# A chunked recurrence: double levels taken apart into single ones that read q in place

## The chip, the cores and the metric

The kernel runs on one core of a Trainium2 chip. A core has five engines with their own instruction streams: PE (TensorE) multiplies matrices, with the loads of its stationary operand shown apart as PEld; DVE (VectorE), ACT (ScalarE) and POOL (GpSimd) work on vectors; SP (SyncE) issues transfers. The metric is the device time of one execution in microseconds (us).

## The reference

The network is one layer of a hybrid block over 2048 positions of width 1024: a normalisation, an input projection to 4608 columns, two branches (a pooling mixer and a gated recurrence), sigmoid gates, an output projection, a convolutional feed-forward part, and a last normalisation. All is fp32. The change touches only the recurrence, with 4 heads of 128 channels. Per head, with the state S (128 x 128):

```
f_t = lb + (1 - lb) * sigmoid(zf_t);   k_t = 1 - f_t;   q_t = silu(zq_t)
S_t = diag(f_t) S_{t-1} + k_t v_t^T
o_t = S_t^T q_t
```

Within a chunk of positions the same is an attention with a decay, summed over the channel c, for s <= t:

```
att[t, s] = sum_c q[t, c] * k[s, c] * f[s+1, c] * ... * f[t, c]
o = att @ v + (q * decay) @ S_of_the_chunk's_start
```

## The kernel before, in words

The 2048 positions are handled as two passes of 1024, and each pass as two blocks of 512 positions (`TB`). In a pass `proj_io` projects the values and the output gate, `mixer` does the other projections (14 units of 7 products, each 4 x 3 matmuls of 128 x 128 x 512, so 1176 matmuls), then the branch projections `pa` and `pb`, then the output rows (`wo`), and `ffn` follows. A weight is split in two fp32r parts, `ops` (L209 on ACT, L210 on DVE), ahead of its use.

The recurrence is `hgrn_task`, one generator for each block and head: 4 blocks x 4 heads = 16 tasks, of which up to three (`N_RUN`) run at once in each pass. Nothing there is a loop of its own. The projections count their matmuls, and at every sixth (`MM_PER_TICK`) a tick lets each task whose `yield n` has run out issue its next step. So a task's instructions lie among those of the projections on every engine. The final order is drawn by the tile framework's scheduler from the order of issue and a timing model. Each engine takes its instructions in order.

In a task the tiles are 128 channels by 512 positions, in four chunks of 128 (`NT`). `d` holds the decays f, `ks` holds k, `q` holds q, and `att` collects the attention of each chunk. The attention is built by levels. At level hh (1, 2, 4, ... 64) a chunk falls into pairs of neighbouring runs of hh positions; a product of `ks` (stationary, 128 columns) with the second runs' q (moving, 64 columns) gives all entries between the runs, a masked copy (`copy_predicated` on DVE, the mask as bytes) takes over the wanted ones into `att`, and then q of the second runs, k of the first runs and the decay of the run are multiplied forward, so that the next level has runs of twice the length. Level 64 needs no mask: its product has 64 stationary columns and ACT copies it (L925).

Before the change levels 0 and 1 (hh = 1, 2) work on copies of q: tiles `q1` and `q2` hold 64 columns for the level's pairs of runs and 64 for the diagonal of the even or the odd positions, side by side, and one product of 128 columns (L915) gives both. Levels 2 and 3, and levels 4 and 5, are done together by `two_levels`: for two chunks at a time, a tile `qm` of 3 x 64 columns gets the near runs (ACT, L867), the half-run copy (POOL, L868) and the multiplied far runs (DVE, L869 and L872), one product of 192 columns per chunk (L876) gives all, three masked copies take it over (L883, L886), and q, k and d go forward by two levels at once (L880, L892 to L898). Level 6 stands alone (L923). L933, L935 and L937 carry q, k and d forward by a single level. Between steps a task yields 3, 4, 4, then 1 + 1 + 5 for each double level, and 4 ticks: 29 up to its last product.

After that a task transposes k (`pk`), updates the state chunk by chunk (`pv`, `ss`), forms the output (`po`), normalises, transposes and spills it (`oh`, L987). The second block's task of a head waits for the first block's state. `pb` reads the spilled outputs. The masks are made by `setup_task` once, in the first pass, on POOL (L576 to L580) and DVE, while `proj_io` runs.

Of the kernel before, what the change touches and what calls it, by code (L numbers as in the profile page):

```python
# [78 lines left out]
def tile_trunk(  # L79
# [482 lines left out]
    def setup_task():  # L562
# [8 lines left out]
        keys = [(h, h, 0, h) for h in (1, 2, 4, 16)]  # L571
        keys += [(8 * h + t, 2 * h, t * h, h) for h in (4, 16) for t in range(2)]
        for key, x, off, w in keys:
            nb = 64 // x
            mf = slot(f"mf{key}", 64)
            pool.memset(mf, 1.0)  # L576
            v = mf.rearrange("p (b h) -> p b h", h=x)
            pool.affine_select(out=v, in_=v, pattern=[[-2 * x, nb], [0, x]],
                               compare_op=ALU.is_ge, fill=0.0, base=-off, channel_multiplier=1)
            pool.affine_select(out=v, in_=v, pattern=[[2 * x, nb], [0, x]],  # L580
                               compare_op=ALU.is_ge, fill=0.0, base=off + w - 1,
                               channel_multiplier=-1)
# [4 lines left out]
        for t in range(2):  # L587
            mf = slot(f"mfd{t}", 64)
            pool.memset(mf, 0.0)
            pool.affine_select(out=mf, in_=mf, compare_op=ALU.not_equal, fill=1.0, base=-t,  # L590
                               pattern=[[-2, 64]], channel_multiplier=1)
            m8 = const.tile([P, 64], U8, tag=f"md{t}", name=f"md{t}")
            yield 2
            dve.tensor_copy(m8, mf)
            masks[-1 - t] = m8.unsqueeze(1)
# [227 lines left out]
    def hgrn_task(b, h, d, q, vd, zd, od):  # L823
        def head_of(src, key):
# [13 lines left out]
        ae, ao = (att.rearrange("p (c b t) -> p c b t", c=NT, t=2)[:, :, :, t] for t in range(2))  # L838
# [4 lines left out]
        dve.tensor_tensor(q1[:, :, 0], qo, do, ALU.mult)  # L843
# [3 lines left out]
        def mask(key, n):  # L847
            m = masks[key]
            return m.unsqueeze(1).to_broadcast([P, n, m.shape[1], m.shape[2]])

        def two_levels(hh):
            nb = P // (4 * hh)
            d5 = d.rearrange("p (c b t h) -> p c b t h", c=NT, t=4, h=hh)
            q5 = q.rearrange("p (c b t h) -> p c b t h", c=NT, t=4, h=hh)
            qv = q.rearrange("p (c b t h) -> p c b t h", c=NT, t=2, h=hh)
            av = att.rearrange("p (c b t h) -> p c b t h", c=NT, t=2, h=hh)
            av2 = att.rearrange("p (c b t h) -> p c b t h", c=NT, t=2, h=2 * hh)
            q2 = q.rearrange("p (c b t h) -> p c b t h", c=NT, t=2, h=2 * hh)
            for i in range(0, NT, 2):
                cc = slice(i, i + 2)  # L860
                mv = (slot(f"qm{b}_{h}_{hh}_{i}")[:, :384]
                      .rearrange("p (c s x) -> p c s x", c=2, s=3))
                near = mv[:, :, 0].rearrange("p c (b h) -> p c b h", h=hh)
                half = mv[:, :, 1].rearrange("p c (b t h) -> p c b t h", t=2, h=hh)
                far = [mv[:, :, 1 + t].rearrange("p c (b h) -> p c b h", h=2 * hh)
                       for t in range(2)]
                act.copy(near, qv[:, cc, :, 1, :])  # L867
                pool.tensor_copy(half[:, :, :, 0, :], q5[:, cc, :, 2, :])  # L868
                dve.tensor_tensor(half[:, :, :, 1, :], q5[:, cc, :, 3, :],  # L869
                                  d5[:, cc, :, 2, 0:1].to_broadcast([P, 2, nb, hh]), ALU.mult)  # L870
                full = [P, 2, nb, 2 * hh]
                dve.tensor_tensor(far[1], far[0], d5[:, cc, :, 1, 0:1].to_broadcast(full),  # L872
                                  ALU.mult)
                pa_ = bank(f"pl{b}_{h}_{hh}_{i}", 384)
                for c in range(2):
                    pe.matmul(pa_[:, c * 192 : c * 192 + 192],  # L876
                              ks[:, (i + c) * P : (i + c + 1) * P],
                              mv[:, c].rearrange("p s x -> p (s x)"), start=True, stop=True)
                ps = pa_.rearrange("p (c s x) -> p c s x", c=2, s=3)
                dve.tensor_tensor(q2[:, cc, :, 1, :], far[1],  # L880
                                  d5[:, cc, :, 0, 0:1].to_broadcast(full), ALU.mult)
                yield 1
                dve.copy_predicated(av[:, cc, :, 1, :], mask(hh, 2),  # L883
                                    ps[:, :, 0].rearrange("p c (b h) -> p c b h", h=hh))
                for t in range(2):
                    dve.copy_predicated(av2[:, cc, :, 1, :], mask(8 * hh + 1 - t, 2),  # L886
                                        ps[:, :, 1 + t].rearrange("p c (b h) -> p c b h", h=2 * hh))
            dd = d.rearrange("p (b t h) -> p b t h", t=4, h=hh)
            qq = q.rearrange("p (b t h) -> p b t h", t=4, h=hh)
            kk = ks.rearrange("p (b t h) -> p b t h", t=4, h=hh)  # L890
            nb *= NT
            dve.tensor_tensor(qq[:, :, 1, :], qq[:, :, 1, :],  # L892
                              dd[:, :, 0, 0:1].to_broadcast([P, nb, hh]), ALU.mult)
            dve.tensor_tensor(dd[:, :, 2, 0:1], dd[:, :, 2, 0:1], dd[:, :, 3, 0:1], ALU.mult)
            dve.tensor_tensor(dd[:, :, 1, 0:1], dd[:, :, 1, 0:1], dd[:, :, 2, 0:1], ALU.mult)
            dve.tensor_tensor(kk[:, :, 0:3, :], kk[:, :, 0:3, :],
                              dd[:, :, 1:4, 0:1].to_broadcast([P, nb, 3, hh]), ALU.mult)
            dve.tensor_tensor(dd[:, :, 0, 0:1], dd[:, :, 0, 0:1], dd[:, :, 1, 0:1], ALU.mult)  # L898

        for lv in (0, 1, 2, 4, 6):  # L900
            hh = 1 << lv
            if lv in (2, 4):
                yield from two_levels(hh)
                yield 5
                continue
# [3 lines left out]
            if lv < 2:  # L909
                qd, ad = ((q1, ae), (q2, ao))[lv]  # L910
                if lv == 1:
                    act.copy(q2[:, :, 0].rearrange("p c (b h) -> p c b h", h=2), qv[:, :, :, 1, :])
                pa_ = bank(f"pl{b}_{h}_{hh}")
                for c in range(NT):
# [715 lines left out]
```

## Time and profile before

| what | value |
|---|---|
| median of 3 runs | 2583.78 us (2582.34 to 2586.46) |
| profiled execution, span from first to last instruction | 2582.7 us |
| PE busy | 2522.6 us, 98% of the span |
| PEld, DVE, ACT, POOL busy | 80%, 77%, 45%, 31% |
| stretch of the recurrence, first pass | 111 to 475 us |
| stretch of the recurrence, second pass | 1396 to 1747 us |

The profile gives no time of its own execution apart from the span; the span lies within the three times. A line of a group reads: source line, engine, operation, result and operands by the names of the tiles, shapes, count, then busy time in us and the mean of one in ns, then the idle time of the engine before them and what ended it. A line of a wait reads: who waited for whom, us in total, how many times, the longest. The timeline gives start and length in us and merges neighbours of one kind. A matmul's record is longer than the pace at which matmuls follow each other, since they overlap. The windows give busy us by engine, then the granted clock of PE, the share of the DMA engines and GB/s.

### The profile page before, as it was taken

The page shows a single profiled execution, that of the slowest core. Times are in us where ns is not written, and L with a number is a line of the kernel's source. Part 1 is how long each engine was busy: PE and PEld are TensorE (multiplying, and loading weights), DVE is VectorE, ACT ScalarE, POOL GpSimd, SP SyncE. Part 2 cuts the span into 40 slices and gives each one's busy share as a digit, 9 for nine tenths or more (in the row PEclk, how much of TensorE's full clock was granted, in tenths as well). Part 3 has the DMA queues.
Part 4 walks back from the last instruction along what each step waited for, and adds up shares of the span by engine and source line. Part 5 has one row for each costly group of instructions (what it writes and reads, how often), then busy time and mean ns, then how long its engine had stood idle before and what let it go on. Part 6 is the DMA issues. An engine that isn't in the chain of part 4 may idle for free.

```text
span 2582.7 us, 35524 instructions
## 1 busy us (share of the span) xinstructions
PE 2522.6 (98%) x11464; PEld 2058.5 (80%) x11464; DVE 1986.3 (77%) x3462; ACT 1171.3 (45%) x2204; POOL 801.8 (31%) x1169
## 2 busy tenths in 40 slices
PE   7999999999999999999999999999999999999998
PEld 6787887888788888778878788888887888887886
DVE  7888778588889787885486887775978888777844
ACT  5334433324645454554364343442355554444623
POOL 3554344001454334451241111200024432325402
PEclk9999999999999999999999999999999999999999
DMA  6778768768788879996454343447453554446942
GB/s 220 258 196 216 209 181 243 236 207 245 192 243 246 224 224 246 252 358 188 132 186 143 102 139 115 123 140 238 145 163 94 155 149 144 145 138 209 365 135 102
DMA packets 252330, 493.74 MB, mean 191 GB/s; under 512 B 26544, under 2 KB 43056, under 8 KB 251824
## 3 DMA queue, kind: packets, MB, share of 16 engines
q1 hardware_dynamic: 186240, 316.75, 38.8%
q0 software_dynamic: 41504, 110.64, 16.7%
q10 hardware_dynamic: 24400, 64.08, 7.3%
q8 instruction: 91, 1.49, 0.2%
q14 instruction: 95, 0.78, 0.1%
HBM read 381.79 MB, written 187.17 MB: 220 GB/s over the span
## 4 chain that ended last, share of the span: by engine, by line
PE 69%; DVE 2%; issue 1%; DMA 1%; ACT 1%; POOL 0%; DVEq 0%; SPq 0%; POOLq 0%; ACTq 0%
PE dn_P L145 15%; PE up_Z L145 13%; PE up_V L145 9%; PE up_X L145 8%; PE wo_P L145 3%; PE gr_Z L145 3%; PE gr_V L145 2%; PE pa L145 2%; PE pb L145 2%; PE gr_X L145 2%; PE io_Z L145 1%; PE fr_Z L145 1%; PE fr_X L145 1%; PE fr_V L145 1%; PE io_V L145 1%
## 5 line engine op out<-in xcount | busy, mean ns | idle before, releaser
L209 ACT CAST ops<-raw 128x512 fp32r<-128x512 f32 x736 | 454.1, 620 | 823.7 <-PE dn_P L145 159.8
L210 DVE TENSOR_TENSOR ops<-raw,ops 128x512 fp32r<-128x512 f32 x736 | 551.7, 753 | 188.1 <-ACT ops L209 180.5
L1423 DVE SCALAR_TENSOR_TENSOR e<-h,cols,e 128x512 f32<-128x512 f32 x176 | 143.3, 818 | 31.2 <-ACT e L1421 26.1
L1421 ACT ACTIVATE e<-h,cols 128x512 f32<-128x512 f32 x176 | 142.6, 814 | 24.1 <-DVE h L1001 17.3
L1426 DVE SCALAR_TENSOR_TENSOR e<-h,cols,e 128x512 f32<-128x512 f32 x176 | 134.7, 774 | 3.0
L819 POOL DMA_DIRECT2D g_P<-dg_P x154 | 83.5, 544 | 114.8 <-PE dn_P L145 77.8
L1108 POOL TENSOR_TENSOR gf_P<-e,e 128x512 f32<-128x512 f32 x44 | 65.0, 1480 | 146.8 <-DVE e L1432 91.0
L1108 POOL TENSOR_TENSOR gf_P<-gf_P,e 128x512 f32<-128x512 f32 x44 | 59.4, 1349 | 72.3 <-DVE e L1432 71.9
L1416 POOL COPY h<-h 128x2 f32<-128x2 f32 x88 | 40.2, 471 | 117.3 <-DVE h L999 113.1
L1418 POOL COPY hist<-h 128x2 f32<-128x2 f32 x88 | 35.6, 405 | 119.9 <-DVE h L1001 118.2
L1430 ACT ACTIVATE e<-e 128x512 f32<-128x512 f32 x88 | 55.6, 631 | 37.7 <-DVE e L1426 37.2
L1001 DVE TENSOR_TENSOR h<-up_u,up_V 128x512 f32<-128x512 f32 x88 | 60.0, 682 | 13.7 <-PE up_V L145 13.2
L1255 ACT ACTIVATE gt<-gt,cols 128x512 f32<-128x512 f32 x48 | 34.8, 725 | 77.6 <-DVE gt L1001 63.6
L1218 POOL TENSOR_TENSOR q<-q,qs 128x512 f32<-128x512 f32 x16 | 21.9, 1366 | 144.3 <-ACT qs L1217 75.6
L1083 DVE TENSOR_TENSOR x<-x,wo_P 128x512 f32<-128x512 f32 x88 | 55.9, 677 | 12.1 <-PE wo_P L145 11.9
L868 POOL COPY qm<-q 128x64 f32<-128x64 f32 x64 | 26.3, 432 | 116.8 <-DVE q L933 30.8
L1083 DVE TENSOR_TENSOR ac<-ac,dn_P 128x512 f32<-128x512 f32 x72 | 46.5, 681 | 17.1 <-PE dn_P L145 17.0
L876 PE MATMUL pl<-qm,k 128*128 128x192 f32 x256 | 47.7, 328 | 6.4 <-DVE qm L872 2.6
L1446 POOL DMA_DIRECT2D dg_P<-gf_P x88 | 50.8, 577 | 7.9 <-POOL gf_P L1108 7.2
L639 POOL TENSOR_TENSOR m_0ss<-m_0ss 128x1 f32<-128x1 f32 x4 | 1.9, 463 | 162.0 <-ACT m_xs L638 162.0
L1035 ACT COPY up_e<-up_X 128x512 f32<-128x512 f32 x44 | 25.8, 586 | 57.2 <-PE up_X L145 54.4
L876 PEld LDWEIGHTS pl<-qm,k 128*128 128x128 f32 x256 | 42.7, 190 | 11.0 <-ACT qm L867 2.5
(1266 smaller groups left out, 8195.6 us busy)
## 6 DMA issues: line engine op xcount, KB each, us to landing
g_P<-dg_P POOLq DMA_DIRECT2D x154, 256.0 KB, 5.9
raw<-in_w_up_t SPq DMA_DIRECT2D x132, 256.0 KB, 3.2
raw<-in_w_in_t SPq DMA_DIRECT2D x98, 256.0 KB, 3.3
dg_P<-gf_P POOLq DMA_DIRECT2D x88, 256.0 KB, 4.0
dg_P<-e SPq DMA_DIRECT2D x66, 256.0 KB, 3.6
raw<-in_w_dn SPq DMA_DIRECT2D x66, 256.0 KB, 3.7
x<-in_x SPq DMA_DIRECT2D x64, 256.0 KB, 5.2
gd<-gt ACTq DMA_DIRECT2D x64, 256.0 KB, 3.0
```

The lines of the kernel that those rows point to most:

```text
L145: count[1] = pe.matmul(*args, **kw)
L209: self.mark = act.copy(hi, v)
L210: dve.tensor_tensor(lo, v, f32(hi), ALU.subtract)
L819: eng.dma_start(t, d)
L876: pe.matmul(pa_[:, c * 192 : c * 192 + 192], ks[:, (i + c) * P : (i + c + 1) * P], mv[:, c].rearrange("p s x -> p (s x)"), start=True, sto ...
L1001: dve.tensor_tensor(dst, t, ps, ALU.add if how == "add" else ALU.subtract)
L1083: dve.tensor_tensor(t, t, ps[j], ALU.add if sg > 0 else ALU.subtract)
L1108: pin(eng.tensor_tensor(t, x0, x1, op))
L1421: in_turn(act.activation(t, h[:, 2:], AF.Identity, bias=col(o_cb + mt), scale=col(o_cw + 4 * MF + mt)))
L1423: in_turn(second(dve.scalar_tensor_tensor(t, h[:, 1 : 1 + TB], col(o_cw + 2 * MF + mt), t, ALU.mult, ALU.add)))
L1426: dve.scalar_tensor_tensor(t, h[:, 0:TB], col(o_cw + mt), t, ALU.mult, ALU.add)
L1430: in_turn(act.activation(g, g, AF.Silu))
```

## The change

All seven levels become single ones. Each level's product reads its moving operand straight from `q`, 64 columns with a step, and the copies `q1`, `q2` and `qm` go. At level 0 the even positions' q, not yet multiplied, goes into one product of 64 columns per chunk, and one masked copy takes the even positions' own (diagonal) entries from it. The odd positions' q, also not multiplied, is copied to `qc`; at level 1, where k of the even positions has been carried forward, one product with `qc` gives an odd position's own entry and its pair, and a second one gives the entries between runs of two. So level 1 has eight matmuls of 64 columns and two masked copies. Levels 2 to 5 have four matmuls of 64 columns, one masked copy over all four chunks, and one multiplication each of q, k and d. Level 6 is as before. A task yields 3 and then 4 ticks after each level, 31 up to its last product. Seven masks are made in place of ten.

```diff
-        keys = [(h, h, 0, h) for h in (1, 2, 4, 16)]
-        keys += [(8 * h + t, 2 * h, t * h, h) for h in (4, 16) for t in range(2)]
-        for key, x, off, w in keys:
+        keys = [(h, h, h) for h in (1, 2, 4, 8, 16, 32)] + [(0, 1, 2)]
+        for key, x, w in keys:
...
-        q1, q2 = (slot(f"q{i}{b}_{h}").rearrange("p (c s x) -> p c s x", c=NT, s=2)
-                  for i in (1, 2))
-        act.copy(q1[:, :, 1], qe)
-        act.copy(q2[:, :, 1], qo)
-        dve.tensor_tensor(q1[:, :, 0], qo, do, ALU.mult)
-        dve.tensor_tensor(qe, qe, de, ALU.mult)
-        dve.tensor_tensor(qo, q1[:, :, 0], de, ALU.mult)
+        qc = slot(f"qc{b}_{h}")[:, : NT * 64].rearrange("p (c x) -> p c x", c=NT)
+        act.copy(qc, qo)
+        dve.tensor_tensor(qo, qo, do, ALU.mult)
+        dve.tensor_tensor(qo, qo, de, ALU.mult)
         yield 3
...
-        def two_levels(hh):
...
-        for lv in (0, 1, 2, 4, 6):
+        for lv in range(7):
             hh = 1 << lv
-            if lv in (2, 4):
-                yield from two_levels(hh)
-                yield 5
-                continue
             nb = P // (2 * hh)
             qv = q.rearrange("p (c b t h) -> p c b t h", c=NT, t=2, h=hh)
             av = att.rearrange("p (c b t h) -> p c b t h", c=NT, t=2, h=hh)
...
+            n = 2 if lv == 1 else 1
+            pa_ = bank(f"pl{b}_{h}_{hh}", NT * n * 64)
+            m = hh if lv == 6 else P
+            for c in range(NT):
+                left = ks[:, c * P : c * P + m]
+                o_ = c * n * 64
                 if lv == 1:
...
+                    pe.matmul(pa_[:, o_ : o_ + 64], left, qc[:, c], start=True, stop=True)
+                    o_ += 64
+                pe.matmul(pa_[:m, o_ : o_ + 64], left, qv[:, c, :, 1 if lv else 0, :],
+                          start=True, stop=True)
+            ps = pa_.rearrange("p (c s x) -> p c s x", c=NT, s=n)
+            if lv == 6:
+                act.copy(av[:hh, :, 0, 1, :], ps[:hh, :, 0])
+            elif lv == 0:
+                dve.copy_predicated(av[:, :, :, 0, :], mask(1), ps[:, :, 0].unsqueeze(3))
+                dve.tensor_tensor(qe, qe, de, ALU.mult)
             else:
...
+                if lv == 1:
+                    dve.copy_predicated(
+                        att.rearrange("p (c b t h) -> p c b t h", c=NT, t=2, h=1)[:, :, :, 1, :],
+                        mask(0), ps[:, :, 0].unsqueeze(3))
+                dve.copy_predicated(av[:, :, :, 1, :], mask(hh),
+                                    ps[:, :, n - 1].rearrange("p c (b h) -> p c b h", h=hh))
```

The lines behind it, which multiply q, k and d forward by one level, stay, and serve all seven levels. Level 0 skips the q line, as before.

More of the change, by code (lines that the diff above doesn't have):

```diff
@@ L578, in setup_task @@
             pool.affine_select(out=v, in_=v, pattern=[[-2 * x, nb], [0, x]],
-                               compare_op=ALU.is_ge, fill=0.0, base=-off, channel_multiplier=1)
+                               compare_op=ALU.is_ge, fill=0.0, base=0, channel_multiplier=1)
             pool.affine_select(out=v, in_=v, pattern=[[2 * x, nb], [0, x]],
-                               compare_op=ALU.is_ge, fill=0.0, base=off + w - 1,
+                               compare_op=ALU.is_ge, fill=0.0, base=w - 1,
                                channel_multiplier=-1)
@@ L586, in setup_task @@
             masks[key] = m8.rearrange("p (b h) -> p b h", h=x)
[L587 to L595, printed above, removed]
         pool.memset(hist, 0.0)
@@ L846, in hgrn_task, with mask @@
+        act.copy(qc, qo)
+        dve.tensor_tensor(qo, qo, do, ALU.mult)
+        dve.tensor_tensor(qo, qo, de, ALU.mult)
         yield 3
-        def mask(key, n):
+        def mask(key):
             m = masks[key]
-            return m.unsqueeze(1).to_broadcast([P, n, m.shape[1], m.shape[2]])
-        def two_levels(hh):
[L852 to L898, printed above, removed]
@@ L900, in hgrn_task @@
-        for lv in (0, 1, 2, 4, 6):
+            return m.unsqueeze(1).to_broadcast([P, NT, m.shape[1], m.shape[2]])
+        for lv in range(7):
             hh = 1 << lv
-            if lv in (2, 4):
-                yield from two_levels(hh)
-                yield 5
-                continue
             nb = P // (2 * hh)
```

18 lines of the change are left out of this document (removed).

## The prediction

> **What bounds the kernel now.** I read the page's first lines and its chain of work first, then the busy time of the two stretches in which the changed code runs, then PE's waits in them, and last the blocks of single matmuls. The first column of the page's group and chain lines is share or busy time as the page names it.
>
> ```profile
> span 2582.7 us, 35524 instructions
> PE 2522.6 (98%) x11464; PEld 2058.5 (80%) x11464; DVE 1986.3 (77%) x3462; ACT 1171.3 (45%) x2204; POOL 801.8 (31%) x1169
> PE 69%; DVE 2%; issue 1%; DMA 1%; ACT 1%; POOL 0%; DVEq 0%; SPq 0%; POOLq 0%; ACTq 0%
> ```
>
> PE is busy for 98% of the span, and every other name on the chain stands at 2% or less. The recurrence runs beside the input projections, from 111 to 475 us in the first pass over the blocks and from 1396 to 1747 us in the second:
>
> ```profile
> core 0: us, PE busy (x) PEld busy (x) DVE busy (x) ACT busy (x) POOL busy (x), PEclk, DMA share, GB/s
> 111.00:475.00 364.00, 351.42 (x1762) 291.74 (x1761) 294.07 (x679) 139.41 (x316) 145.03 (x150) 1.00 0.75 211
> 1396.00:1747.00 351.00, 347.58 (x1757) 291.04 (x1755) 258.05 (x667) 142.01 (x315) 55.08 (x86) 1.00 0.41 126
> ```
>
> PE idles for 12.6 us in the first stretch and 3.4 us in the second, 16.0 us in all. So in just these stretches PE sets the pace: a microsecond added to its work is a microsecond of the span, and work taken from DVE, ACT or POOL is worth no more than the idle time that it ends. What PE waited for there (us in total, times, longest), of the first stretch and then, in a fence of its own, of the second:
>
> ```profile
> PE pl L915 <- DVE q L843: 3.9, 2, 2.2
> PE pl L876 <- DVE qm L872: 2.6, 3, 2.0
> PE pl L876 <- ACT ops L209: 2.0, 2, 1.3
> PE pl L876 <- ACT gr_e L1035: 1.9, 1, 1.9
> PE pl L915 <- DVE k L935: 0.4, 1, 0.4
> ```
>
> ```profile
> PE pl L915 <- DVE q L843: 1.2, 1, 1.2
> ```
>
> The recurrence's own products account for 12.0 us of the 16.0.
>
> **The change on PE.** For each of the 16 tasks (four blocks, four heads) the products are, before: levels 0 and 1 with four matmuls of 128 moving columns each (L915), two double levels with four of 192 each (L876), level 6 with four of 64 (L923). That is 20 matmuls and 2816 moving columns. After: levels 0 and 2 to 6 with four of 64 each, level 1 with eight of 64: 32 matmuls and 2048 columns. Fewer columns, more matmuls. Which counts is read from the lines of the loads (PEld) and the products:
>
> ```profile
> L915 PEld LDWEIGHTS pl<-q,k x256: 186/192/338, 137.8 to 1691.2; 128*128 128x128 f32 x128
> L915 PE MATMUL pl<-q,k x256: 269/275/423, 137.8 to 1691.3; 128*128 128x128 f32 x128
> L876 PEld LDWEIGHTS pl<-qm,k x256: 186/190/192, 155.1 to 1714.3; 128*128 128x128 f32 x128
> L876 PE MATMUL pl<-qm,k x256: 323/326/402, 155.3 to 1714.5; 128*128 128x192 f32 x128
> L923 PEld LDWEIGHTS pl<-q,k x128: 132/138/139, 175.3 to 1717.2; 128*64 128x64 f32 x128
> L923 PE MATMUL pl<-q,k x128: 221/222/271, 175.3 to 1717.3; 128*64 128x64 f32 x128
> ```
>
> The three durations in ns are the least, the median and the largest. Each line counts twice the matmuls (16 tasks x 4 x 2 levels = 128 at L915, and 256 records): an fp32 product is two passes, and each pass has its own load. Moving columns from 64 to 128 to 192 take the median from 222 to 275 to 326 ns, 53 and 51 ns for each 64. Stationary columns from 64 to 128 take the load from 138 to 190 ns, 52 ns for 64. So a load of 128 columns streams for 2 x 52 = 104 ns beside a fixed part, and a pass over 64 columns for 53 ns. The new passes keep the load of 128 (their left side is the full 128 columns of `ks`, at all levels but 6) and have only 53 ns of streaming to hide it behind. What one pass costs in a block comes from the timeline (start, length):
>
> ```profile
> 148.01 1.95 PE L915 MATMUL pl<-q,k 128*128 128x128 f32 x16
> ```
>
> ```profile
> 171.05 2.76 PE L876 MATMUL pl<-qm,k 128*128 128x192 f32 x16
> 175.35 1.15 PE L923 MATMUL pl<-q,k 128*64 128x64 f32 x16
> ```
>
> Taking off the last pass's duration and dividing by the others: (1.95 - 0.275)/15 = 112 ns for 128 columns, (2.76 - 0.326)/15 = 162 ns for 192, (1.15 - 0.222)/15 = 62 ns for 64 on 64. Is a load really held to about 107 ns, or does it only look so because those passes move 128 columns? The one place where two full loads follow each other with nothing streaming is behind an idle stretch of PE:
>
> ```profile
> 176.42 0.19 PEld L145 LDWEIGHTS fr_X<-x_f0h,ops 128*128 128x128 f32 x1
> 176.53 0.19 PEld L145 LDWEIGHTS fr_X<-x_f0l,ops 128*128 128x128 f32 x1
> ```
>
> The second load starts 0.11 us after the first. I therefore price every new pass with 128 stationary columns at 112 ns, the row of equal load, and keep 62 ns (the L923 row, equal stream) as the other end.
>
> Sum per task: before, 16 x 0.112 + 16 x 0.162 + 8 x 0.062 = 4.88 us. After, 56 passes x 0.112 + 8 x 0.062 = 6.77 us. Difference +1.89 us, times 16 tasks = **+30.2 us on PE**, on the path. Of it, level 0 costs nothing (8 passes before and after, at the load's pace), level 1 gives 8 more passes = 0.90, and four levels of 8 passes in place of 16 long ones give 3.58 - 2.59 = 0.99. Seven blocks stand among the projections before and after, so the price of getting in and out of a block does not change.
>
> The moving operand now lies in `q` itself, with steps of two elements (level 0) or pairs out of four (level 1). No product of before streams such an operand. Below: no cost. Above: a stream of double length, 106 ns, would still end within the load's 112, so both ends give 0; only more than double would show.
>
> **The change off PE.** The rows of DVE, ACT and POOL (count, busy, mean ns):
>
> ```profile
> L886 DVE COPY_PREDICATED at<-m,pl 128x128 f32<-128x128 uint8 x128 | 32.9, 290 | 0.6
> L927 DVE COPY_PREDICATED at<-m,pl 128x256 f32<-128x256 uint8 x32 | 24.3, 759 | 0.0
> L935 DVE TENSOR_TENSOR k<-k,f 128x256 f32<-128x256 f32 x48 | 23.7, 494 | 0.0
> L896 DVE TENSOR_TENSOR k<-k,f 128x384 f32<-128x384 f32 x32 | 23.1, 723 | 0.0
> L883 DVE COPY_PREDICATED at<-m,pl 128x128 f32<-128x128 uint8 x64 | 18.3, 290 | 14.8 <-PE pl L876 14.6
> L872 DVE TENSOR_TENSOR qm<-qm,f 128x128 f32<-128x128 f32 x64 | 18.0, 300 | 0.1
> L880 DVE TENSOR_TENSOR q<-qm,f 128x128 f32<-128x128 f32 x64 | 17.9, 289 | 0.2
> L933 DVE TENSOR_TENSOR q<-q,f 128x256 f32<-128x256 f32 x32 | 14.8, 464 | 3.3 <-PE pl L923 2.8
> L869 DVE TENSOR_TENSOR qm<-q,f 128x64 f32<-128x64 f32 x64 | 14.1, 255 | 0.0
> L867 ACT COPY qm<-q 128x128 f32<-128x128 f32 x64 | 16.1, 295 | 3.3 <-DVE at L886 2.8 <-ACT gt L1255 0.4
> L868 POOL COPY qm<-q 128x64 f32<-128x64 f32 x64 | 26.3, 432 | 116.8 <-DVE q L933 30.8 <-DVE q L892 21.6 <-PE pl L915 12.3
> ```
>
> Gone: 34 DVE instructions of the double levels per task and one of the two diagonal copies. The six largest of DVE's, shown above (L886, L896, L883, L872, L880, L869), make 124.3 us, and what else goes comes on top. In their place each of four levels has one predicated copy of 256 (between 290 ns, the copy of 128, and 759, the copy of 256 in runs of one or two elements; I take 2 x 290 = 580, since runs are four or longer), one q of 464, one k of 494 and a short one under 300: 1.84 us x 64 = 118 us. DVE's net is a gain, and it lies beside PE, since DVE is busy for 294 of 364 us in its fuller stretch. ACT loses the L867 copies (16.1 us) and POOL the L868 ones (26.3 us), both far from full. I price all this at nothing by itself; its worth is the waits that it ends. Three masks fewer are made during the output-gate projection of the first pass. PE's one wait there names DVE, not POOL, so I price their four selects at nothing:
>
> ```profile
> PE io_Z L145 <- DVE io_u L1153: 1.9, 1, 1.9
> ```
>
> Those waits: the 6.5 us that L876 waited were for operands copied and multiplied in the very step of the product (`qm`); the new products read what the step before, four ticks earlier, left in `q` and `ks`. The 5.1 us at L915 for L843 were for the prologue on a full DVE; level 0 now has one instruction less in front of it. Both ends for the 12.0 us: all of it goes, or none, or as much again comes, because every single level now waits for DVE's k and q of the one before. Level 1 after level 0 has that shape already, and it waited 0.4 us in 16 tasks (L915 behind L935). Nearest to that row, I take 8 of the 12 us as won.
>
> A task takes 3 + 7 x 4 = 31 ticks to its last product where it took 29, two ticks later; a tick is six of the projections' matmuls, and the whole first stretch, 364 us, holds 1176 of them, so two ticks are under 12 x 0.31 = 3.7 us. The last head's output and the stage that reads it:
>
> ```profile
> 487.90 0.68 ACT L987 ACTIVATE oh<-pt,cols 128x512 f32<-128x512 f32 x1
> ```
>
> ```profile
> 522.36 0.39 PE L145 MATMUL pb<-oTs_0h,ops 128*128 128x512 f32 x1
> ```
>
> 34 us lie between; a shift of 4 us, and PE's longer work that shifts both, cost nothing.
>
> **Sum.** +30.2 - 8 = +22.2 us on the profiled span of 2582.7. That span is 1.1 us under the median of 2583.78 (the three times lie between 2582.34 and 2586.46), so against the median the forecast is 2606. A difference of 0.2%, 5 us, is about what a measurement of this kernel can tell from no change.
>
> **Rivals.** *The stream sets the pass, and the kernel gets faster.* If a pass over 64 columns costs 62 ns whatever its load, a task's products take 64 x 0.062 = 3.97 us, 0.91 less than before; times 16 that is -15 us, with the waits -23: 2561. Against it stand the two loads 0.11 us apart. The point that decides is where 56 passes + 0.50 us equal 4.88 us: 78 ns for each pass, or 87 with the 8 us of waits (8 us over 16 x 56 passes, 9 ns). The Trainium skill's page "TensorE: Matmul & The Clock Gate" has a table of gaps (section "Back-to-back issue gap") by which the gap falls with the moving columns alone, 134 cycles at 128 and about 60 at 64; scaled to the 112 ns measured here that would be an estimate of 50 ns a pass, and this rival's outcome. The same page's section "LDWEIGHTS (loading the stationary operand)" makes the load last P/1.2 ns, 107 at 128 columns, and the trace's 0.11 us is on that side. I give this rival 7 in 100.
>
> *The waits go altogether.* Then all 16.0 us of idle and the half-speed stretches that followed two of them are won:
>
> ```profile
> 401.50:404.90 3.40, 1.16 (x8) 0.76 (x7) 3.40 (x7) 3.04 (x8) 2.65 (x2) 0.99 1.08 353
> 404.90:408.30 3.40, 3.40 (x17) 3.21 (x16) 3.40 (x8) 1.88 (x4) 0.89 (x2) 0.50 1.02 199
> 1425.40:1428.80 3.40, 3.03 (x7) 2.46 (x8) 3.40 (x9) 0.32 (x1) 0.00 (x0) 0.51 0.31 99
> ```
>
> After a stretch with 1.16 us of work in 3.40 the granted clock was 0.50 for the next 3.4 us, which costs up to 1.7; the two of them make 3.4. 30.2 - 19.4 = +10.8, or 2595. With passes of 104 ns, the load's streaming alone, in place of 112 (56 x 16 x 8 ns = -7.2 us), it is 2587, no change that can be told: 5 in 100.
>
> *PE slows itself.* Two tasks often stand back to back (the x16 rows). A level-1 pair is then 32 passes, 3.6 us in which the array streams 53 of every 112 ns. If that counts as idle, each of 8 pairs is followed by a half-speed stretch, 8 x 1.7 = 13.6 us: 2620, and with the waits not won 2628. Against it, the clock dropped where PE was busy for a third of a stretch, and here loads and passes run on. The skill's page just named (section "Part 1: The HAM clock gate") says that such a monitor looks at activity in windows of 3413 ns, and the 3.4 us here agree; no row shows how it counts a pass that waits for its load. 8 in 100.
>
> **Chances.** Forecast 0.80, from 2590 (all waits won, the pass between 104 and 112) to 2622 (waits not won, and a few half-speed stretches); stream-bound 0.07; no change 0.05; slowed further 0.08. The range 2590 to 2622 is the forecast's own. Faster 0.07, same 0.05, slower 0.88.
>
> **What would show it.** The new product's lines: loads at 190 ns, passes at about 222, blocks of eight that last 7 x 0.112 + 0.222 = 1.01 us and not 0.66, and 16 of them in level 1. PE's busy time in the two stretches up by about 30 us, its idle there at or below 8, DVE's busy time down. The prediction is wrong if blocks of eight last under 0.85 us, if `pl` waits for DVE's k at every level, or if the clock column falls below 1.00 in these stretches.

## The result, and the profile after

The changed kernel takes 2606.82 us (median; 2605.88 to 2607.32) against 2585.12 us before it (2582.34 to 2588.49; a fourth time has moved that median from 2583.78). The ratio is 1.0082, with a 95% interval of 1.0069 to 1.0094: slower by 0.8%, and the interval stays clear of the 0.2% that a measurement of this kernel can tell. The forecast was 2606, which was +22.2 us on 2583.78; the medians are 21.7 us apart.

The page of the changed kernel: its span, PE's row and the head of the chain of work.

```profile
span 2605.5 us, 35726 instructions
PE 2548.7 (98%) x11848; PEld 2087.3 (80%) x11848; DVE 1944.6 (75%) x3155; ACT 1149.5 (44%) x2108; POOL 767.5 (29%) x1098
PE 44%; DVE 1%; ACT 0%; issue 0%; POOL 0%; DVEq 0%; POOLq 0%; ACTq 0%
```

The span grew by 22.8 us and PE's busy time by 26.1, while DVE lost 41.7 us of work, ACT 21.8 and POOL 34.3. The chain that the page follows covers 45% of the span here and 74% before, so its shares are not compared. Work was taken from the engines that had room and put on the one that has none. There are 384 more matmul records, 16 tasks x 24, as counted.

Where the time lies is read from the same two stretches, bounded by events: from the recurrence's first projection product to the end of the projections (columns: stretch, its length, busy us and count of PE, PEld, DVE, ACT and POOL, granted clock, share of the DMA engines, GB/s), kernel after:

```profile
111.80:484.40 372.60, 366.00 (x1956) 308.77 (x1954) 270.91 (x527) 129.32 (x270) 127.01 (x118) 0.99 0.73 208
1407.80:1770.00 362.20, 360.85 (x1950) 305.19 (x1949) 238.74 (x513) 130.83 (x268) 37.90 (x53) 1.00 0.39 123
```

Against before (364.0 and 351.0 us long, 351.42 and 347.58 busy) PE is busy for 27.9 us more and idles for 8.0 us where it idled for 16.0. The later tasks run past the end of the projections, so from here on I count to the first product of the stage that reads the outputs (`pb`). The sums of the two stretches so bounded, of before and then of after:

```profile
sum 808.90, PE 791.66 PEld 658.24 DVE 595.31 ACT 309.56 POOL 203.68; mean PE 395.83 PEld 329.12 DVE 297.66 ACT 154.78 POOL 101.84
```

```profile
sum 832.10, PE 820.20 PEld 689.22 DVE 552.22 ACT 287.03 POOL 169.77; mean PE 410.10 PEld 344.61 DVE 276.11 ACT 143.52 POOL 84.89
```

The stretches are 23.2 us longer, which is the whole growth of the span: 28.5 us more PE work, and 5.3 us less idle time (17.2 before, 11.9 after). What PE waited for, after: the four longest waits of the first stretch, then all three of the second:

```profile
PE pl L852 <- DVE k L822: 3.5, 1, 3.5
PE pt L924 <- DVE ot L918: 1.7, 1, 1.7
PE po L907 <- DVE ss L897: 1.7, 1, 1.7
PE pm L796 <- DVE pl_0l L600: 0.7, 1, 0.7
```

```profile
PE pt L924 <- DVE ot L918: 1.7, 1, 1.7
PE pl L852 <- DVE k L822: 0.9, 1, 0.9
PE gr_X L145 <- ACT gr_e L974: 0.5, 1, 0.5
```

The waits for `qm` are gone with `qm`. The prologue's is still there: L822 is its multiplication of k, and level 0's product waits 4.4 us in all for it, where it waited 5.1 us for q. No level waits for the level before it. The state and output products wait 5.1 us; before's list for its first stretch has one such line, and that for its second none (its 0.6 us for the transposition of k, `pk`, is gone after):

```profile
PE pt L985 <- DVE ot L979: 1.2, 1, 1.2
```

The new products in the list of groups (busy us, mean ns, then idle before them), and DVE's masked copy of four chunks:

```profile
L852 PE MATMUL pl<-q,k 128*128 128x64 f32 x768 | 104.6, 273 | 4.4 <-DVE k L822 4.4
L850 PE MATMUL pl<-qc,k 128*128 128x64 f32 x128 | 23.8, 268 | 0.0
L852 PE MATMUL pl<-q,k 128*64 128x64 f32 x128 | 10.0, 227 | 0.0
L865 DVE COPY_PREDICATED at<-m,pl 128x256 f32<-128x256 uint8 x80 | 39.6, 495 | 31.4 <-PE pl L852 31.1
```

There are 768 + 128 = 896 = 16 x 56 passes with 128 stationary columns, each recorded with about 270 ns though it moves 64 columns. And two blocks in the timeline of after (start, length), one of 16 passes and one of 8, each between two matmuls of a projection:

```profile
160.12 0.40 PE L145 MATMUL gr_V<-x_B220l,ops 128*128 128x512 f32 x1
160.35 1.89 PE L852 MATMUL pl<-q,k 128*128 128x64 f32 x16
162.06 0.48 PE L145 MATMUL gr_V<-x_B220h,ops 128*128 128x512 f32 x1
162.37 0.39 PE L145 MATMUL gr_V<-x_B221h,ops 128*128 128x512 f32 x1
...
305.79 0.40 PE L145 MATMUL gr_Z<-x_T23h,ops 128*128 128x512 f32 x1
306.02 1.00 PE L852 MATMUL pl<-q,k 128*128 128x64 f32 x8
306.83 0.48 PE L145 MATMUL gr_V<-x_T10h,ops 128*128 128x512 f32 x1
307.15 0.40 PE L145 MATMUL gr_V<-x_T10l,ops 128*128 128x512 f32 x1
```

By the blocks' own records the pace is (1.89 - 0.275)/15 = 108 ns a pass in the long block, (1.00 - 0.275)/7 = 104 in the short one. From one projection product to the next, less the 0.23 us that a projection product takes anyway, a block costs 162.06 - 160.12 - 0.23 = 1.71 us, or 306.83 - 305.79 - 0.23 = 0.81. The product behind a block takes longer than 0.23 us (162.37 - 162.06 = 0.31), so the whole cost is read one product further on: 162.37 - 160.12 - 0.46 = 1.79 and 307.15 - 305.79 - 0.46 = 0.90, which is 112 ns a pass in both. The block of 16 passes with 128 moving columns that the prediction shows for before (148.01) stands between these two products:

```profile
147.78 0.40 PE L145 MATMUL gr_Z<-x_T33h,ops 128*128 128x512 f32 x1
...
150.04 0.39 PE L145 MATMUL gr_Z<-x_T40l,ops 128*128 128x512 f32 x1
```

It costs 150.04 - 147.78 - 0.46 = 1.80 us. A pass with 64 moving columns costs what one with 128 costs.

### The profile page after: what moved, and what is told of

Its sections match the earlier page's. It is cut to its first block, busy times and chain, and to the rows that moved or that the text cites. A ratio compares the mean times of both kernels' runs of the same rounds, so it can differ in the third digit from the quotient of the medians.

```text
span 2605.5 us, 35726 instructions
## 1 busy us (share of the span) xinstructions
PE 2548.7 (98%) x11848; PEld 2087.3 (80%) x11848; DVE 1944.6 (75%) x3155; ACT 1149.5 (44%) x2108; POOL 767.5 (29%) x1098
## 3 DMA queue, kind: packets, MB, share of 16 engines
q0 software_dynamic: 41504, 110.64, 16.5%
## 5 line engine op out<-in xcount | busy, mean ns | idle before, releaser
L210 DVE TENSOR_TENSOR ops<-raw,ops 128x512 fp32r<-128x512 f32 x736 | 560.7, 765 | 216.9 <-ACT ops L209 207.0
L852 PEld LDWEIGHTS pl<-q,k 128*128 128x128 f32 (+1 forms) x896 | 110.1, 186 | 14.6 <-POOL w44s L405 3.9
L852 PE MATMUL pl<-q,k 128*128 128x64 f32 (+1 forms) x896 | 114.6, 267 | 4.4 <-DVE k L822 4.4
L865 DVE COPY_PREDICATED at<-m,pl 128x256 f32<-128x256 uint8 x80 | 39.6, 495 | 31.4 <-PE pl L852 31.1
L1022 DVE TENSOR_TENSOR ac<-ac,dn_P 128x512 f32<-128x512 f32 x72 | 46.6, 682 | 16.6 <-PE dn_P L145 16.5
L872 DVE TENSOR_TENSOR q<-q,f 128x256 f32<-128x256 f32 x96 | 51.4, 536 | 4.6 <-PE pl L852 4.6
```

The lines of the kernel that those rows point to most:

```text
L210: dve.tensor_tensor(lo, v, f32(hi), ALU.subtract)
L852: pe.matmul(pa_[:m, o_ : o_ + 64], left, qv[:, c, :, 1 if lv else 0, :], start=True, stop=True)
L1022: dve.tensor_tensor(t, t, ps[j], ALU.add if sg > 0 else ALU.subtract)
```

## The experiments

The theory: a pass lasts as long as the load of its 128 stationary columns, whatever it moves up to 128, so 24 more passes in each task cost PE their loads, and the idle time that the simpler levels end does not pay for it. The first rival: the stream sets the pass, and the loss comes from elsewhere (the strided operand, late operands). The second: the single levels are starved or badly placed, and a few ticks of lead would mend them.

All the ratios are against the kernel before. Each is taken against runs of before made together with that kernel's, whose medians lie between 2584.6 and 2586.9, so it is not the quotient of this table's medians. The stretches are those that end at `pb`, from one profiled execution of each kernel; that execution lies up to 5.1 us off its kernel's median (2592.27 us in the last row), so differences of 2 or 3 us between the rows' stretches show little.

| kernel | median us | ratio, 95% interval | stretches us | PE busy | PE idle |
|---|---|---|---|---|---|
| before | 2585.12 | | 808.9 | 791.7 | 17.2 |
| after | 2606.82 | 1.0082 (1.0069 to 1.0094) | 832.1 | 820.2 | 11.9 |
| 64 stationary columns | 2596.14 | 1.0041 (1.0026 to 1.0057) | 818.2 | 801.7 | 16.5 |
| 128 moving columns | 2612.08 | 1.0106 (1.0088 to 1.0125) | 835.3 | 821.1 | 14.2 |
| level 1 as one product | 2598.32 | 1.0052 (1.0038 to 1.0066) | 821.1 | 807.2 | 13.9 |
| new low levels, old double ones | 2593.29 | 1.0026 (1.0016 to 1.0036) | 818.3 | 806.4 | 11.9 |
| old low levels, single ones above | 2594.96 | 1.0032 (1.0020 to 1.0044) | 816.1 | 802.7 | 13.4 |
| after, 3 more ticks ahead of the levels | 2608.82 | 1.0091 (1.0077 to 1.0105) | 829.3 | 820.5 | 8.8 |
| before, with leads | 2617.81 | 1.0119 (1.0105 to 1.0134) | 837.2 | 800.1 | 37.1 |
| joined level 1, double levels, leads | 2609.63 | 1.0094 (1.0082 to 1.0106) | 833.8 | 798.7 | 35.1 |
| the same without leads | 2584.46 | 0.9997 (0.9986 to 1.0007) | 808.6 | 793.5 | 15.1 |
| before, one tick ahead of the double products | 2587.13 | 1.0006 (0.9995 to 1.0016) | 814.7 | 795.9 | 18.8 |

### Half the stationary columns

```diff
-            m = hh if lv == 6 else P
+            m = 64
...
-                    pe.matmul(pa_[:, o_ : o_ + 64], left, qc[:, c], start=True, stop=True)
+                    pe.matmul(pa_[:m, o_ : o_ + 64], left, qc[:, c], start=True, stop=True)
...
-                dve.copy_predicated(av[:, :, :, 1, :], mask(hh),
-                                    ps[:, :, n - 1].rearrange("p c (b h) -> p c b h", h=hh))
+                dve.copy_predicated(av[:m, :, :, 1, :], mask(hh)[:m],
+                                    ps[:m, :, n - 1].rearrange("p c (b h) -> p c b h", h=hh))
```

> The changed kernel with 64 stationary columns in place of 128 at every level; the moving operands, their steps in q and all waits stay. The entries of the second 64 key positions of each chunk are left out at the levels that had 128. If the load of the stationary side sets a pass, the 56 passes of a task fall from 108 to about 62 ns: 56 x 16 x 0.046 = 41 us less than the changed kernel's 2607, so about 2566, under the kernel before. If the stream of 64 columns sets it (for instance because a stepped operand is read at half pace, 2 x 53 = 106 ns), the pass stays at 108 and the time at 2607.

Measured: 2596.14 us. The line of 896 of its `pl` passes (the 128 others, of level 1, have a median of 221), least, median and largest in ns, and the sum of its stretches:

```profile
L852 PE MATMUL pl<-q,k x896: 218/222/367, 140.0 to 1734.4; 128*64 128x64 f32 x180
```

```profile
sum 818.20, PE 801.74 PEld 643.00 DVE 558.28 ACT 286.82 POOL 175.98; mean PE 400.87 PEld 321.50 DVE 279.14 ACT 143.41 POOL 87.99
```

The moving operand, its steps and the number of matmuls are those of after; only the load is halved, and the passes fall from about 273 to 222 ns and PE's busy time by 18.5 us. The load sets the pass. The gain is far below what 50 ns on 896 passes would give, 45 us, and the time far above the 2566 expected. The timeline of this kernel shows why, PE first, then the loads of the same place:

```profile
171.86 0.40 PE L145 MATMUL ur_X<-x_f4h,ops 128*128 128x512 f32 x1
172.19 1.15 PE L852 MATMUL pl<-q,k 128*64 128x64 f32 x16
173.26 0.50 PE L145 MATMUL ur_Z<-x_T30h,ops 128*128 128x512 f32 x1
...
157.01 0.40 PE L145 MATMUL gr_Z<-x_T43h,ops 128*128 128x512 f32 x1
157.33 0.68 PE L852 MATMUL pl<-q,k 128*64 128x64 f32 x8
157.94 0.50 PE L145 MATMUL gr_V<-x_B220h,ops 128*128 128x512 f32 x1
```

```profile
171.63 0.19 PEld L145 LDWEIGHTS ur_X<-x_f4h,ops 128*128 128x128 f32 x1
172.19 1.01 PEld L852 LDWEIGHTS pl<-q,k 128*64 128x64 f32 x16 [0.36 <-PE ur_V L145]
```

After, block for block:

```profile
159.88 0.19 PEld L145 LDWEIGHTS gr_V<-x_B220l,ops 128*128 128x128 f32 x1
160.12 1.99 PEld L852 LDWEIGHTS pl<-q,k 128*128 128x128 f32 x16
```

A load of 128 columns behind others of 128 starts 0.24 us after the one before it, beside the streaming matmul. The load of 64 starts 0.56 us after the one before it, 0.36 us idle. So 16 narrow passes cost 173.26 - 171.86 - 0.23 = 1.17 us and 8 of them 157.94 - 157.01 - 0.23 = 0.70: 59 ns a pass and some 0.23 us for entering and leaving, where 16 and 8 wide passes (1.71 and 0.81) give 112 ns a pass and nothing fixed. (One product further on, at 173.60 and 158.28, they cost 1.28 and 0.81, with 0.34 us fixed.) Blocks gain about 0.5 or 0.1 us, not 0.8 or 0.4. PE's idle time also grew, from 11.9 to 16.5 us. The Trainium skill's page "TensorEngine Tiling (Array Packing)" says in its section "Key Properties" that a change of tiling mode drains TensorE; the 0.36 us of idle agree with a drain, and the page gives no duration for it. That a load of 64 columns among loads of 128 is such a change is not shown here.

### Twice the moving columns

```diff
+            wide = lv not in (1, 6)
...
+                if wide:
+                    pe.matmul(pa_[:, c * P : (c + 1) * P], left, q[:, c * P : (c + 1) * P],
+                              start=True, stop=True)
+                    continue
```

> The changed kernel with 128 moving columns (the whole chunk of q, without steps) in place of 64 at levels 0 and 2 to 5; the masked copies take the wanted columns out of the wider result. 40 passes per task are twice as wide. If the load sets a pass, it goes from 108 to the 112 ns of the kernel before: 40 x 16 x 0.004 = 2.6 us more, about 2609. If the stream sets it, each pass gets 53 ns longer: 34 us more, about 2641. If the steps in q set it, the passes stay near 107 and the time near 2607.

Measured: 2612.08 us. Its passes and its stretches:

```profile
L850 PE MATMUL pl<-q,k x640: 270/275/417, 142.2 to 1741.4; 128*128 128x128 f32 x160
```

```profile
sum 835.30, PE 821.12 PEld 688.91 DVE 550.69 ACT 286.79 POOL 169.02; mean PE 410.56 PEld 344.45 DVE 275.34 ACT 143.40 POOL 84.51
```

Twice the columns on 640 passes, and PE is busy for 0.9 us more, no more than one half-speed stretch makes. If the stream set the pace, 640 x 53 ns = 34 us would have come. It also reads whole chunks, without steps, and is no faster for it: the strided operand costs nothing that shows. The other 2.3 us of the stretches are idle time.

### Level 1 as one product

```diff
-        qc = slot(f"qc{b}_{h}")[:, : NT * 64].rearrange("p (c x) -> p c x", c=NT)
-        act.copy(qc, qo)
+        qc = slot(f"qc{b}_{h}").rearrange("p (c s x) -> p c s x", c=NT, s=2)
+        act.copy(qc[:, :, 0], qo)
...
-                    pe.matmul(pa_[:, o_ : o_ + 64], left, qc[:, c], start=True, stop=True)
-                    o_ += 64
+                    pe.matmul(pa_[:, o_ : o_ + P], left, qc[:, c].rearrange("p s x -> p (s x)"),
+                              start=True, stop=True)
+                    continue
```

> The changed kernel with level 1's two products of 64 columns joined to one of 128 (a copy of the second runs' q by ACT, made a step earlier, stands beside qc). Eight passes fewer per task, the same number of columns. If the count of loads sets PE's time: 8 x 16 x 0.108 = 14 us less, about 2593. If the count of columns does, or if the loss is in waits and not in passes: 2607, or a little more for the added copy.

Measured: 2598.32 us. The same columns in half the passes:

```profile
sum 821.10, PE 807.19 PEld 675.33 DVE 557.48 ACT 292.50 POOL 168.91; mean PE 403.60 PEld 337.67 DVE 278.74 ACT 146.25 POOL 84.46
```

PE is busy for 13.0 us less than after, 102 ns for each of the 128 passes saved. Splitting level 1's product was nearly half of the change's cost on PE. The median fell by 8.5 us where 14 were expected; in the stretches 2.0 us of the gain came back as idle time.

### The parts alone

The first kernel has after's levels 0, 1 and 6 and before's double levels; the second has before's levels 0 and 1 and single levels above.

```diff
-        for lv in range(7):
+        def two_levels(hh):
...
+        for lv in (0, 1, 2, 4, 6):
             hh = 1 << lv
+            if lv in (2, 4):
+                yield from two_levels(hh)
```

> The changed kernel's levels 0, 1 and 6 with the double levels of the kernel before (levels 2+3 and 4+5, products of 192 columns): the change of levels 0 and 1 alone. By passes that cost 112 ns at 128 stationary columns: 8 passes more per task than before, 16 x 8 x 0.112 = +14 us, about 2599 against 2585 before. If the loss lies in taking the double levels apart alone, 2585 to 2588.

```diff
-        for lv in (0, 1, 2, 4, 6):
+        for lv in range(7):
...
+            elif lv < 6:
+                pa_ = bank(f"pl{b}_{h}_{hh}", 256)
+                for c in range(NT):
+                    pe.matmul(pa_[:, c * 64 : (c + 1) * 64], ks[:, c * P : (c + 1) * P],
+                              qv[:, c, :, 1, :], start=True, stop=True)
```

> The kernel before with its double levels taken apart into single ones, levels 0, 1 and 6 as before: the other part of the change alone. By passes: 32 x 0.112 - 16 x 0.162 = 0.99 us per task, +16 us, less the 6.5 us that PE waited for the operands of the double levels: about 2594. With e4 it should add up to the change's +22. If the loss lies in levels 0 and 1 alone: 2579 to 2585.

Measured: 2593.29 and 2594.96 us, ratios 1.0026 and 1.0032. The sums of the stretches:

```profile
sum 818.30, PE 806.37 PEld 674.38 DVE 587.22 ACT 299.84 POOL 196.72; mean PE 403.18 PEld 337.19 DVE 293.61 ACT 149.92 POOL 98.36
```

```profile
sum 816.10, PE 802.72 PEld 671.30 DVE 562.23 ACT 297.16 POOL 173.51; mean PE 401.36 PEld 335.65 DVE 281.11 ACT 148.58 POOL 86.76
```

The low levels alone add 14.7 us to PE's busy time, the single levels alone 11.1: together 25.8 of the 28.5 that both cost. These figures hold the time that PE lost at half speed. In the first kernel it ran at about half its clock in two places:

```profile
139.70:149.50 9.80, 8.49 (x28) 7.46 (x29) 8.30 (x18) 0.00 (x0) 0.87 (x1) 0.50 0.71 256
248.70:252.40 3.70, 3.70 (x11) 3.20 (x12) 3.70 (x14) 0.72 (x1) 0.33 (x1) 0.54 1.08 215
```

That loses 8.49 x 0.50 + 3.70 x 0.46 = 5.9 us, where before lost 3.2 and after 4.5 (both are worked out below, 1.2 apart). The second kernel's granted clock is 1.00 in both stretches, and it lost none. At full clock the parts are 14.7 - 2.7 = 12.0 and 11.1 + 3.2 = 14.3 us, together 26.3 of the 28.5 - 1.2 = 27.3 of both. Each part is a loss by itself, about a third of a per cent. Each ends idle time as well (5.3 and 3.8 us), and both together end only 5.3, as if some idle time were won by either. That is not shown: the spans of the same executions, 2593.1 and 2592.3 against 2582.7 us, grow by 10.4 and 9.6, nearly the 22.8 of both.

### A lead for the waits

```diff
-        yield 3
+        yield 6
```

> The changed kernel with 6 ticks in place of 3 between a task's preparation and its first product. If the wait of the first product for DVE's k (3.5 us and 0.9 us in the trace) and the half-speed stretch behind it (6.8 us, worth up to 3.4) are real losses that more lead ends, about 2600 to 2602. If the wait only moves to the next level's product, 2607.

Measured: 2608.82 us, with an interval that overlaps that of after. The wait that it was meant to end, in its first stretch, is 4.1 us in all, in two places (start, length, and in brackets the idle time ahead of it):

```profile
139.63 2.14 PE L852 MATMUL pl<-q,k 128*128 128x64 f32 x16 [0.77 <-DVE k L822]
415.51 1.54 PE L852 MATMUL pl<-q,k 128*128 128x64 f32 x6 [3.38 <-DVE k L822]
```

The work of PE is that of after (820.5 us). The first of these products waits 3.50 us in after, so the lead took most of that wait away; but a later task's product, ahead of which after has no wait, now waits 3.38 us. Three ticks, 18 projection products, moved the wait and did not end it. So the single levels did not lose for want of a few ticks.

The same leads on the kernel before, and on a kernel with the joined level 1 and the old double levels; the double-level product gets two ticks more:

```diff
-        yield 3
+        yield 6
...
+                yield 2
                 pa_ = bank(f"pl{b}_{h}_{hh}_{i}", 384)
```

> The kernel before with 6 ticks in place of 3 ahead of a task's first product and 2 more ticks between the making of a double level's operands and its product. If PE's waits for these operands (6.5 us) and for the preparation (5.1 us, and two half-speed stretches worth up to 3.4) can be ended by lead, up to 15 us less, 2570 to 2580. If the waits only move, because DVE is behind as a whole where they arise, 2585 as before, as the lead in e6 gave nothing to the changed kernel.

> Level 1's two products joined to one of 128 columns as in e3, the double levels of the kernel before, and the leads of e7. PE has the passes of the kernel before (8 + 8 of 128, 16 of 192, 8 of 64 per task), DVE has one masked copy and ACT one copy less per task. By passes alone 2585; if lead and the lighter DVE end waits, 2570 to 2580.

Measured: 2617.81 and 2609.63 us, ratios 1.0119 and 1.0094. None of the times expected (2570 to 2585) was above before's. Both lose by idle time and by the half-speed clock behind it. The first has 37.1 us of idle time; the place in its first stretch that holds the largest part of it:

```profile
366.00:396.00 30.00, 18.25 (x60) 14.35 (x60) 9.89 (x18) 5.91 (x10) 7.69 (x8) 0.76 0.58 165
```

PE idles for 11.75 of these 30 us, and the granted clock falls to 0.76. DVE, ACT and POOL stand idle for most of it too, so it is no engine's load. The trace shows them waiting for each other. The longest idle time of PE in it, 6.8 us, is for a multiplied `qm`, which stands on DVE behind a pooling sum (`s`, L792). That sum starts at 382.92, after 4.0 us put down to the transfer that writes a gate to memory (`gd<-gt`); before that DVE waited 6.0 us for ACT's `ops`, and ACT 4.5 us for POOL's `w100s`. The kernel takes `s`, the gates and `w100s` from one pool of buffers (`slot`), so they may have waited for a free buffer; no run tested that. The waits for `qm` were not ended either (first stretch):

```profile
PE pl L877 <- DVE qm L872: 8.8, 4, 6.8
```

The last two runs separate the parts: the joined kernel with its leads taken out again, and before with a single tick ahead of the double products.

```diff
-        yield 6
+        yield 3
...
-                yield 2
```

> e8 without its leads: level 1 as one product of 128 columns, the double levels of the kernel before, the yields of the kernel before. PE has the passes of the kernel before, so its busy time in the two stretches, with half-speed time taken off, should be the 788 us of the kernel before within 3 us. DVE has one masked copy and ACT one copy less per task. If the leads made e8's loss, 2580 to 2588; if the joined form itself did, about 2610 as e8.

```diff
+                yield 1
                 pa_ = bank(f"pl{b}_{h}_{hh}_{i}", 384)
```

> The kernel before with one tick between the making of a double level's operands and its product, nothing else: a third of e7's change. PE's busy time in the two stretches should stay at the 788 us of the kernel before. If the 6.5 us of waits for those operands can be ended by one tick, about 2580. If a longer task by itself makes PE wait elsewhere, as e7's 37 us of idle suggest, 2590 to 2600.

Measured: 2584.46 us (ratio 0.9997) and 2587.13 us (1.0006, between the two times expected); both intervals hold 1. The sum of the joined kernel:

```profile
sum 808.60, PE 793.48 PEld 660.16 DVE 585.71 ACT 304.94 POOL 203.63; mean PE 396.74 PEld 330.08 DVE 292.86 ACT 152.47 POOL 101.81
```

So it was the leads that lost in the joined kernel, 20 us of idle time. Without them it has before's number of passes with 128 stationary columns, 10 us less work on DVE and 5 less on ACT in the stretches, and before's time: work taken off DVE and ACT, at the same number of passes, is worth nothing that can be told here. With one tick, the waits of the double levels' products fell from 6.5 us to 0.5, but another wait grew, that of level 0 for the prologue's q (3.9 us in before's first stretch):

```profile
PE pl L916 <- DVE q L843: 10.3, 5, 4.3
```

No kernel tried is faster than the one before.

## Why the prediction was right

**PE sets the pace in the two stretches: right.** The span grew by what the stretches grew, and what DVE, ACT and POOL lost did not come back as time.

**A pass with 128 stationary columns costs the same whatever it moves up to 128: right, with its size.** It was priced at 112 ns; read to the second product behind them, blocks of after cost 112 ns a pass, and before's with 128 moving columns the same. The Trainium skill's "TensorE: Matmul & The Clock Gate" puts such a load at P/1.2, an estimate of 107 ns for 128 columns (section "LDWEIGHTS (loading the stationary operand)"); the 112 ns are 5% above it. Halving the load shortened the pass, doubling the stream did not lengthen it. The rival by which the stream sets the pass is refuted. One reading on the way to it was off: the two loads 0.11 us apart stand not behind an idle stretch of PE but right behind level 6's block at 175.35, which lasts until 176.50.

**+30.2 us on PE: a tenth too high.** PE's busy time grew by 28.5, of which 1.2 is half-speed time (below); at full clock it grew by 27.3. The missing 3 us are not in the price of a pass, and no run shows where they are. Level 1's part was put at +0.90 us a task, 14.4 in all: the low levels alone cost 12.0 at full clock, and joining the product gave 13.0 back. Levels 2 to 5 were put at +0.99, 15.9 in all: alone they cost 14.3, and beside the new low levels 820.2 - 806.4 + 5.9 - 4.5 = 15.2.

**Half-speed stretches: there, and of about the old size.** Two places of after, each with the stretch ahead of it, and as the last two lines the level-1 blocks of two tasks back to back and the 3.4 us behind them:

```profile
136.40:139.80 3.40, 0.59 (x3) 0.16 (x1) 3.40 (x3) 1.47 (x3) 3.32 (x3) 1.00 1.07 389
139.80:146.60 6.80, 6.11 (x22) 5.57 (x23) 6.40 (x16) 0.00 (x0) 1.85 (x2) 0.50 1.08 346
491.40:494.80 3.40, 1.74 (x6) 0.57 (x4) 1.10 (x2) 1.68 (x7) 0.00 (x0) 0.99 1.06 402
494.80:498.20 3.40, 2.80 (x7) 2.26 (x8) 2.51 (x7) 0.60 (x5) 2.38 (x3) 0.50 0.56 206
153.50:156.90 3.40, 3.40 (x31) 3.33 (x30) 3.15 (x6) 0.72 (x1) 1.27 (x1) 1.00 0.04 13
156.90:160.30 3.40, 3.40 (x16) 2.79 (x15) 3.40 (x8) 1.83 (x3) 1.73 (x2) 1.00 1.00 323
```

Half of the busy time at 0.50 is lost: (6.11 + 2.80)/2 = 4.46 us after, (3.40 + 3.03)/2 = 3.22 before, so +1.24 that the sum does not have. Both drops follow idle time of PE. The block of level 1, full of passes that wait for loads, kept a clock of 1.00, and so did the 3.4 us behind it: the rival by which PE slows itself did not come. The prediction said that a clock below 1.00 in these stretches would make it wrong; the first stretch's mean is 0.99, but from idle time and not from the passes, and the test should have been put that way.

**8 of 12 us of waits won: the mechanism right in part, the size too high.** The 6.5 us ahead of the double levels' products went, as forecast; that all of it was for `qm` is more than the list says, which puts 2.6 down to `qm` and 3.9 to ACT's `ops` and `gr_e`. Of the prologue's 5.1, 0.7 went. In before, k was done only 0.3 us ahead of the q that the list names (137.35 and 137.69 us, the product starts at 137.84), so one instruction less could win little there, and in after k came later still: the two `ops` ahead of it took DVE 3.48 us and k itself 1.48, where they took 2.42 and 0.41 in before. POOL added weights beside them almost without a pause in after, and stood idle from 135.87 to 138.23 us in before; that this slowed DVE was not tested. The state and output products wait 3.9 us more than before. The net is 5.3 us. The step that failed is taking most of the prologue's 5.1 us as won.

**No wait from level to level, the stepped operand free, two ticks free: right.** Neither of after's lists of waits has the first (the kernel with the joined level 1 waits so for 1.2 us in its first stretch, the one with the old low levels for 0.7), twice the columns without steps was no faster, and the stretches end as late as PE's own work makes them.

**DVE lighter, worth nothing: right.** DVE's busy time fell by 41.7 us in all. Its masked copy took 495 ns, not 580.

**The records: wrong.** Forecast were passes of about 222 ns; they are 273. The blocks of eight took 1.00 us as forecast (1.01), so only the reading of one record was wrong: it lasts with the load, not with its own stream.

The terms were off in opposite directions: 27.3 in place of 30.2, +1.2 for the clock which was not in the sum, and 5.3 in place of 8. They make the 23.2 us by which the stretches grew, against the sum of 22.2 and the span's 22.8. That the total came within 1 us owes something to these misses cancelling; by its terms alone the forecast was good to about 3 us.

What stays open is why the leads bring about the chain of waits in the first stretch, what slows DVE ahead of L822's k, and where the 3 us of PE work are that the sum had too many.

## What to carry to other kernels

Count passes of the array, not moving columns: where each pass brings a new stationary operand of 128 columns, moving 64 costs what 128 cost, so two short products with one left side should be one product, even if a copy has to put their operands side by side. Operations saved on an engine beside the bounding one are worth only the waits that they end, and a wait that is ended in one place can come back in another. Read the cost of a block of short matmuls from the starts of its neighbours, up to the second one behind it, and not from its records. Take the time at half speed out of busy times before comparing them: here it turned the order of the two parts round.

## What the runs showed of the chip that was not expected

A matmul record with a new load lasts by the longer of load and stream: 273 ns with 128 stationary and 64 moving columns, 275 with 128 and 128, 326 with 128 and 192, 222 with 64 and 64.

A block of products with 64 stationary columns among products with 128 costs about 0.23 us to enter and leave, 0.34 with the product behind it: 16 of them take 1.17 us and 8 take 0.70. That eats most of the gain of a narrower load in a short block.

PE at the load's pace, streaming for about half of the time (an estimate: 53 ns of each 112), kept a granted clock of 1.00 for 3.4 us and the 3.4 us behind them. In the two places of after it was 0.50 behind 3.4 us with 0.59 and with 1.74 us of busy time.
